# Projection front with ten unscaled k tiles, spread rescaling, and the last token tile ended in two halves

## The chip, the cores and the metric

The kernel runs on one core of a Trainium2 chip. The metric is the device time of one execution in microseconds, as the median of three runs. The times of the profile come from one further execution that was recorded instruction by instruction. PE is TensorE, DVE VectorE, ACT ScalarE, POOL GpSimd and SP SyncE, whose queue issues most of the transfers.

## The reference, cut to what matters

One decoder block on 512 tokens of width 2048. An RMS norm, one wide input projection, two token mixers (an mLSTM with 8 heads and a gated DeltaNet with 16 heads, both computed in chunks of 64 tokens), one output projection, and in the kernel's entry the residual and a last RMS norm.

```python
u = _rmsnorm(h, norm_w)                      # x * rsqrt(mean(x*x) + eps) * norm_w
proj = jnp.matmul(u, w_in)                   # q, k, v, o, z, gates of both mixers
i_pre = _softcap(ml_i + ml_i_bias)           # gates: 8 + 8 + 16 + 16 columns of proj
logf = jax.nn.log_sigmoid(_softcap(ml_f + ml_f_bias))
h_a = _mlstm_chunkwise(q, k, v, i_pre, logf) # then norm, sigmoid(o), silu(z)
beta = jax.nn.sigmoid(dn_b)
g = -jnp.exp(dn_a_log) * jax.nn.softplus(dn_a + dn_dt_bias)
h_b = _gated_delta_chunkwise(dq, dk_, dv_, beta, g)
y_a = jnp.matmul(h_a, w_out[:ML_WIDTH])
y_b = jnp.matmul(h_b, w_out[ML_WIDTH:])
return jax.nn.sigmoid(gate_a) * y_a + jax.nn.sigmoid(gate_b) * y_b
```

The factor rsqrt(mean(x*x) + eps) is one number for each token. It can be put on x before the projection, or on the projection's result.

## The kernel before

**Products in parts.** Each float32 operand is split into a high part rounded to fp32r and the rest: u into `uh` and `ul`, a weight tile `wr` into `wh` (a cast on ScalarE, L140) and `wl` (a subtraction on VectorE, L143). A product is three matmuls: uh with wh, ul with wh, uh with wl (L257 to L259). The 2048 input columns are 16 k tiles of 128; a weight tile holds 2 k tiles by 256 columns, 256 KB, and is loaded by SyncE (L172) in the order of a list `plan`. A projection block gives 256 columns for 512 tokens, in two banks `pj` of PSUM, with 96 matmuls of 512 columns.

**The front.** x comes in eight transfers of 512 KB, two halves for each of four tiles of 128 tokens (L270), ahead of the weights. For each token tile ScalarE squares one half and VectorE the other with a running sum (L297, L299); from these come the token factors `rs` (L301 to L304, the root on GpSimd), and both engines scale their half of x in place (L290, L292). Then `make_u` turns one k tile of x by four transposes (L313, tile `put`) and splits it into `uh` and `ul` (L314, L315), with the norm's weight as a factor by partition. `first_block` runs that two k tiles ahead of the first projection block (the mLSTM's queries), and puts between its products those of the gate columns (L324, L325, bank `pgr`), eight k tiles behind. At its end ScalarE copies the gates out (`gr0`, L356) and spills the queries (L349) to DRAM.

**Behind the front.** Three more projection blocks follow without a pause of TensorE. Beside them run generators that the blocks' `tick` calls step on. `gates()` transposes the gate columns back to tokens (L401, tile `pgt`), computes the decays on small columns `sml` in a long chain of VectorE instructions (L405 to L434), transposes these to rows (L443 to L445, tiles `pri`, `prf`, `prg`) and scans them (L454 to L457). `u_sums()` forms sums and differences of halves of u (L373 to L378, tile `X`, each k pair one pass of 1024 and four of 256 columns) and splits them (L382 and L384). They feed the stage that takes most of the kernel's time (L578 to L580), which forms four block products by seven.

**Order.** TensorE's order is the order in which the code is written. On the other engines a scheduler orders by priorities when the program is built; after that every engine works its queue strictly in that order, and a waiting instruction holds all behind it.

**The tail.** The last block of the output projection ends token tile by token tile: for tile c the products of the last six k tiles (18 matmuls of 512 columns, L1391 to L1393, bank `py`), then `done_c(c)`: gate and residual on VectorE (L1692, L1693), square on ScalarE (L1694), the sum (L1696), the root on GpSimd (L1697), the first 1024 output columns scaled on ScalarE (L1699) and sent by SyncE (L1700). `leave(c)` scales the other 1024 columns on VectorE (L1705, L1706) and sends them by ScalarE's queue (L1707).

Of the kernel before, what the change touches and what calls it, by code (L numbers as in the profile page):

```python
# [15 lines left out]
P = 128  # L16
# [12 lines left out]
GLAG = 8  # L29
# [29 lines left out]
def hybrid_body(  # L59
# [91 lines left out]
    plan = [("i", (ML_Q, ML_K)[a] + b * NB, k) for a, b in QK for k in range(0, KT, KP)]  # L151
# [10 lines left out]
    limit = [nfront]  # L162

# [11 lines left out]
    def split_next():  # L175
        raw, nk, n = raws[len(parts)]
        with tc.high_priority(offset=2 * PRIO if len(parts) > SAHEAD else 0):
            hi = wp.tile([P, nk, n], F32R, tag="wh", name="wh", bufs=NSPL)
            lo = wp.tile([P, nk, n], F32R, tag="wl", name="wl", bufs=NSPL)
            with ExitStack() as first:  # L180
                if not parts:
                    first.enter_context(behind("V"))
                    first.enter_context(behind("A"))
                elif len(parts) == 1:
                    first.enter_context(tc.issue_after(done["V"]))
                    first.enter_context(tc.issue_after(done["A"]))
                split_hi(hi, raw)
                split_lo(lo, raw, hi)
        parts.append((hi, lo))

    def prepare(i):
        while len(raws) < min(limit[0], i + RAHEAD + 1):
            load_raw()
        while len(parts) < min(limit[0], i + SAHEAD + 1):
            split_next()
# [50 lines left out]
    def proj_cm(col0, before=None):  # L246
        ps = [psj.tile([P, S], F32, tag="pj", name="pj") for _ in range(2)]
        for kt0 in range(0, KT, KP):
            hi, lo = next_w("i", col0, kt0)
            if before is not None:  # L250
                for k in range(KP):
                    before(kt0 + k)
            for j in range(2):
                for k in range(KP):
                    kt = kt0 + k
                    wsl = slice(j * P, (j + 1) * P)
                    T.matmul(ps[j], hi[:, k, wsl], uh[:, kt, :], start=(kt == 0), stop=False)  # L257
                    T.matmul(ps[j], hi[:, k, wsl], ul[:, kt, :], start=False, stop=False)  # L258
                    T.matmul(ps[j], lo[:, k, wsl], uh[:, kt, :], start=False, stop=(kt == KT - 1))  # L259
# [6 lines left out]
    xts = []  # L266
    for c in range(NC):
        xt = p0.tile([P, D], F32, tag=f"x{c}", name=f"xt{c}")
        for i in range(2):
            nc.sync.dma_start(xt[:, i * HD:(i + 1) * HD], x[c * P:(c + 1) * P, i * HD:(i + 1) * HD])  # L270
        xts.append(xt)
    for _ in range(2):
        load_raw()
# [3 lines left out]
    wgh, wgl = wgp[:, :, 0:48], wgp[:, :, 64:112]  # L277
    G.memset(wgp[:, :, 48:64].bitcast(F32), 0.0)
    taps = []
    ss = p0.tile([P, NC, 2], F32, tag="ss", name="ss")  # L280
    rs = p0.tile([P, NC], F32, tag="rs", name="rs")
    mhalf = cp.tile([P, NC], F32, tag="mhalf", name="mhalf")
    G.memset(mhalf, -0.5)
    half = cp.tile([P, 2, NC], F32, tag="half", name="half")
    G.memset(half, 0.5)
    sq, done = {}, {}

    def scale_x(c):
        with tc.issue_after(sq["V"]):
            newest["V"] = V.tensor_scalar(out=xts[c][:, 0:HD], in0=xts[c][:, 0:HD], scalar1=rs[:, c:c + 1], scalar2=None,  # L290
                                        op0=ALU.mult).ins
        newest["A"] = A.mul(xts[c][:, HD:D], xts[c][:, HD:D], rs[:, c:c + 1]).ins  # L292

    for c in range(NC):
        xt = xts[c]
        jk = p0.tile([P, HD], F32, tag="jk", name="jk", bufs=2)
        A.activation(jk, xt[:, 0:HD], AF.Square, accum_out=ss[:, c, 0:1])  # L297
        jv = p0.tile([P, HD], F32, tag="jv", name="jv", bufs=2)
        sq["V"] = V.scalar_tensor_tensor(out=jv, in0=xt[:, HD:D], scalar=1.0, in1=xt[:, HD:D], op0=ALU.mult, op1=ALU.mult,  # L299
                                         accum_out=ss[:, c, 1:2]).ins  # L300
        V.tensor_tensor(out=rs[:, c:c + 1], in0=ss[:, c, 0:1], in1=ss[:, c, 1:2], op=ALU.add)  # L301
        V.tensor_scalar(out=rs[:, c:c + 1], in0=rs[:, c:c + 1], scalar1=1.0 / D, scalar2=EPS,
                        op0=ALU.mult, op1=ALU.add)
        G.tensor_tensor(out=rs[:, c:c + 1], in0=rs[:, c:c + 1], in1=mhalf[:, c:c + 1], op=ALU.pow)  # L304
        if c:
            scale_x(c - 1)
    scale_x(NC - 1)

    def make_u(kt):
        pool, tg = ((psw, "wk"), (pso, "o"))[kt % 2]  # L310
        pt = pool.tile([P, S], F32, tag=tg, name="put")
        for c in range(NC):
            T.transpose(pt[:, c * P:(c + 1) * P], xts[c][:, kt * P:(kt + 1) * P], ident)  # L313
        done["A"] = A.activation(uh[:, kt, :], pt, AF.Copy, scale=normc[:, kt:kt + 1]).ins  # L314
        done["V"] = V.scalar_tensor_tensor(out=ul[:, kt, :], in0=pt, scalar=normc[:, kt:kt + 1],  # L315
                                           in1=uh[:, kt, :].bitcast(F32), op0=ALU.mult, op1=ALU.subtract).ins

    UA = 2
# [1450 lines left out]
```

## Time and profile before

| | us |
|---|---|
| median of three runs | 2154.34 (2153.77 to 2154.91) |
| the profiled execution's own time | 2153.98 |
| its span, first to last instruction | 2152.2 |
| PE busy | 2122.7 (99%) |
| DVE busy | 1710.5 (79%) |
| ACT busy | 1041.6 (48%) |
| first product of the first block | 20.64 |
| last product of the kernel | 2142.57 |

Busy time is the union of an engine's instructions; it says nothing of which engine the end waits for. The span is 1.8 us shorter than the execution's own time, since what precedes the first and follows the last instruction is not in it. In rows of the timeline the first number is an instruction's start from the span's begin, the second its duration; instructions of one engine overlap a little, so that the next one may start before the duration is over. The granted clock (PEclk) is a share of TensorE's full 2.4 GHz.

### The profile page before, as it was taken

Reading aid. Unit: us, or ns where it says so; the run is one execution under the profiler, and the core shown is the slowest. Engines: PE = TensorE matmul, PEld = TensorE weight load, DVE = VectorE, ACT = ScalarE, POOL = GpSimd, SP = SyncE. Lnnn points to the kernel's source line nnn. Section 1 sums busy time; section 2 is a strip of 40 time slices with the busy share of each in tenths; the row PEclk is TensorE's granted clock in tenths of the full one; section 3 lists DMA queues with packets and bytes.
Section 4 is the critical chain, followed back from the end, with each engine's and each line's share of the span. In section 5 each row is a group of like instructions: output and inputs, shape, how many; then the busy total and the mean of one; then the engine's idle time right before and its main releaser. Section 6 shows DMA issues by size and latency. Waiting matters only on the chain.

```text
span 2152.2 us, 31876 instructions
## 1 busy us (share of the span) xinstructions
PE 2122.7 (99%) x10544; PEld 1760.0 (82%) x10544; DVE 1710.5 (79%) x2973; ACT 1041.6 (48%) x1994; POOL 431.5 (20%) x651
## 2 busy tenths in 40 slices
PE   6999999999999999999999999999999999999998
PEld 5888888888888888888888888888888888887886
DVE  5888888788888778777757887887887878569887
ACT  5444444445444444444445545556455464345345
POOL 0000000000004000000002335234233263233221
PEclk9999999999999999999999999999999999999999
DMA  5456676667678767776767777767786677778895
GB/s 162 117 193 191 211 215 196 220 202 227 203 228 243 243 195 223 237 231 195 254 201 176 186 178 185 166 181 188 178 222 171 167 183 209 198 231 278 242 301 230
DMA packets 447143, 444.20 MB, mean 206 GB/s; under 512 B 197121, under 2 KB 303842, under 8 KB 446850
## 3 DMA queue, kind: packets, MB, share of 16 engines
q1 hardware_dynamic: 377618, 337.22, 54.7%
q0 software_dynamic: 24752, 72.90, 10.9%
q10 hardware_dynamic: 44608, 32.06, 4.7%
q8 instruction: 82, 1.34, 0.3%
q14 instruction: 83, 0.68, 0.1%
HBM read 348.66 MB, written 97.58 MB: 207 GB/s over the span
## 4 chain that ended last, share of the span: by engine, by line
PE 94%; DMA 2%; DVE 2%; SPq 1%; issue 1%; ACT 0%; ACTq 0%; DVEq 0%; POOLq 0%; POOL 0%
PE ps L579 17%; PE ps L578 17%; PE ps L580 17%; PE pj L257 9%; PE pj L259 9%; PE pj L258 9%; PE py L1391 2%; PE py L1393 2%; PE py L1392 2%; PE pk L909 1%; PE pqk L979 1%; PE pnum L1197 1%; PE pw L1071 1%; PE po L1086 1%; DMA wr<-in_w_in_dram 0%
## 5 line engine op out<-in xcount | busy, mean ns | idle before, releaser
L140 ACT CAST wh<-wr 128x512 fp32r<-128x512 f32 (+1 forms) x522 | 373.7, 717 | 442.3 <-PE pj L258 233.7
L143 DVE TENSOR_TENSOR wl<-wr,wh 128x512 fp32r<-128x512 f32 (+1 forms) x522 | 439.2, 842 | 171.5 <-ACT wh L140 167.6
L257 PE MATMUL pj<-uh,wh 128*128 128x512 f32 x896 | 376.4, 420 | 0.0
L259 PE MATMUL pj<-uh,wl 128*128 128x512 f32 x896 | 351.3, 392 | 0.0
L258 PE MATMUL pj<-ul,wh 128*128 128x512 f32 x896 | 350.6, 391 | 0.0
L579 PE MATMUL ps<-wl,uh 128*128 128x512 f32 x752 | 292.6, 389 | 0.0
L578 PE MATMUL ps<-wh,uh 128*128 128x512 f32 x752 | 292.6, 389 | 0.0
L580 PE MATMUL ps<-wh,ul 128*128 128x512 f32 x752 | 292.5, 389 | 0.0
L140 ACT CAST wh<-t 128x1024 fp32r<-128x1024 f32 x120 | 126.3, 1053 | 298.4 <-PE ps L580 189.9
L578 PE MATMUL ps<-wh,suh 128*128 128x512 f32 x624 | 242.9, 389 | 0.1
L579 PE MATMUL ps<-wl,suh 128*128 128x512 f32 x624 | 242.8, 389 | 0.0
L580 PE MATMUL ps<-wh,sul 128*128 128x512 f32 x624 | 242.7, 389 | 0.0
L533 POOL DMA_DIRECT2D t_d<-ts x104 | 56.6, 545 | 922.3 <-DVE ts L520 854.0
L140 ACT CAST wh<-ts 128x512 fp32r<-128x512 f32 x240 | 148.4, 618 | 186.8 <-DVE ts L538 157.6
L143 DVE TENSOR_TENSOR wl<-t,wh 128x1024 fp32r<-128x1024 f32 x120 | 146.9, 1224 | 82.1 <-ACT wh L140 81.6
L259 PEld LDWEIGHTS pj<-uh,wl 128*128 128x128 f32 x896 | 168.4, 188 | 37.3
L257 PEld LDWEIGHTS pj<-uh,wh 128*128 128x128 f32 x896 | 169.3, 189 | 30.1
L258 PEld LDWEIGHTS pj<-ul,wh 128*128 128x128 f32 x896 | 169.5, 189 | 28.3
L143 DVE TENSOR_TENSOR wl<-ts,wh 128x512 fp32r<-128x512 f32 x240 | 164.5, 686 | 32.8 <-ACT wh L140 31.3
L579 PEld LDWEIGHTS ps<-wl,uh 128*128 128x128 f32 x752 | 141.2, 188 | 29.7 <-DVE wl L143 0.4
L578 PEld LDWEIGHTS ps<-wh,uh 128*128 128x128 f32 x752 | 141.1, 188 | 29.4
L580 PEld LDWEIGHTS ps<-wh,ul 128*128 128x128 f32 x752 | 141.1, 188 | 29.1
(334 smaller groups left out, 3763.8 us busy)
## 6 DMA issues: line engine op xcount, KB each, us to landing
wr<-in_w_in_dram SPq DMA_DIRECT2D x744, 256.0 KB, 3.7
wr<-in_w_out_dram SPq DMA_DIRECT2D x138, 256.0 KB, 4.7
t_d<-ts POOLq DMA_DIRECT2D x104, 256.0 KB, 3.7
wr<-t_d SPq DMA_DIRECT2D x104, 256.0 KB, 3.8
xt<-in_x_dram SPq DMA_DIRECT2D x8, 512.0 KB, 7.1
tg_d<-X ACTq DMA_DIRECT2D x16, 256.0 KB, 4.7
tg_d<-to ACTq DMA_DIRECT2D x16, 256.0 KB, 4.4
v<-v_d SPq DMA_DIRECT2D x8, 512.0 KB, 6.1
```

The source lines that it names most:

```text
L140: newest["A"] = A.copy(hi, src).ins
L143: newest["V"] = V.tensor_tensor(out=lo, in0=src, in1=hi.bitcast(F32), op=ALU.subtract).ins
L257: T.matmul(ps[j], hi[:, k, wsl], uh[:, kt, :], start=(kt == 0), stop=False)
L258: T.matmul(ps[j], hi[:, k, wsl], ul[:, kt, :], start=False, stop=False)
L259: T.matmul(ps[j], lo[:, k, wsl], uh[:, kt, :], start=False, stop=(kt == KT - 1))
L533: queue.dma_start(t2_d[b % 2, i], ts[:, 0, :])
L578: T.matmul(ps[t], ah, hi, start=(g == "A" and i == 0), stop=False, skip_group_check=True)
L579: T.matmul(ps[t], ah, lo, start=False, stop=False, skip_group_check=True)
L580: T.matmul(ps[t], al, hi, start=False, stop=(i == KH - 1), skip_group_check=True)
L1391: T.matmul(ps[c], uh[:, kt, tsl], hi, start=(kt == ks[0]), stop=False)
L1392: T.matmul(ps[c], uh[:, kt, tsl], lo, start=False, stop=False)
L1393: T.matmul(ps[c], ul[:, kt, tsl], hi, start=False, stop=(kt == ks[-1]))
```

## The change

**Front.** x is one tile `xt` for all tokens and is loaded in five pieces of columns (borders 0, 256, 512, 1024, 1280, 2048), with the first weight tiles between them. The first `KU` = 10 k tiles are transposed and split unscaled and go into banks of their own (`rawp`, `rawg`). The squares stand in three pieces of columns between the steps of the first block (`hook`), on both engines in an order that the code writes out. When `rs` is there, x of k tiles 10 to 15 is scaled in place (`scale_x`), and the factors are turned into a row of tokens `rrow` by four matmuls (`turn_row`). With it the unscaled banks are brought to scale as they leave (`gr0`, `qk0`), and the second banks are added. `uh` and `ul` of the first ten k tiles are formed anew for the blocks that follow, pair by pair (`rescale`: sum and factor, `rescaled`: split); for k tiles 4 to 9 the transposed x is kept for that in the place of x in `xt`, which takes one more pass of ScalarE. The second block takes its k tiles in the order 10 to 15, 0 to 9. `gates()` starts four ticks later.

**Tail.** The products of the last token tile's last six k tiles are written in two halves of 256 columns, `done_c` runs for each half, and `whole(c)` scales the first 1024 columns in two pieces; the last tile leaves in four transfers of 256 KB, three by SyncE and one by ScalarE's queue.

The diff, cut to its core:

```diff
+KU = 10
+    KS = {q: list(range(0, KT, KP)) for q in QK}
+    KS[QK[1]] = list(range(KU, KT, KP)) + list(range(0, KU, KP))
...
-        xt = p0.tile([P, D], F32, tag=f"x{c}", name=f"xt{c}")
+    xt = p0.tile([P, NC, D], F32, tag="x", name="xt")
+    XC = [0, 256, 512, 1024, 1280, D]
+    for n in range(len(XC) - 1):
+        o = slice(XC[n], XC[n + 1])
+        with behind("S") if n else ExitStack():
+            newest["S"] = nc.sync.dma_start(xt[:, :, o], xv[:, :, o]).ins
+        if n in (0, 1, 3, 4):
+            with behind("S"):
+                load_raw()
...
+    def turn_row(diag):
+        pr = psw.tile([P, S], F32, tag="wk", name="prow")
+        for c in range(NC):
+            T.matmul(pr[:, c * P:(c + 1) * P], ones, diag[:, c, :], start=True, stop=True)
+        A.copy(rrow, pr)
...
+    def split_u(kt, pt):
+        hi, lo = uh[:, kt, :], ul[:, kt, :]
+        if kt < 4 or kt >= KU:
+            A.activation(hi, pt, AF.Copy, scale=normc[:, kt:kt + 1])
+            V.scalar_tensor_tensor(out=lo, in0=pt, scalar=normc[:, kt:kt + 1], in1=hi.bitcast(F32), op0=ALU.mult, op1=ALU.subtract)
+        else:
+            f = whole(kt - 4, 1)[:, 0]
+            A.activation(f, pt.rearrange("p (c t) -> p c t", t=P), AF.Copy, scale=normc[:, kt:kt + 1])
+            split_hi(hi.rearrange("p (c t) -> p c t", t=P), f)
+            split_lo(lo.rearrange("p (c t) -> p c t", t=P), f, hi.rearrange("p (c t) -> p c t", t=P))
+    def rescale(p):
...
+        if p < 2:
+            f = uf[p] = by_chunk(p0.tile([P, KP, S], F32, tag="uf", name="uf", bufs=2))
+            V.tensor_tensor(out=f, in0=hi.bitcast(F32), in1=lo.bitcast(F32), op=ALU.add)
+        else:
+            f = uf[p] = whole(KP * p - 4, KP)
+        V.tensor_tensor(out=f, in0=f, in1=rr, op=ALU.mult)
...
+    def hook(n):
...
+        if n == 7:
+            split_hi(wgh, wg)
+            split_lo(wgl, wg, wgh)
+            square(A, 2, 2)
+            square(V, 2, 3)
+            token_factors()
+        if n == 8:
+            scale_x(KU, KU + 2)
+            gps["diag"] = factor_row()
...
+        if n + 2 < KT:
+            split_u(n + 2, turn_x(n + 2))
...
+        if n in (11, 13, 15):
+            rescale((n - 11) // 2)
+        if n in (12, 14):
+            rescaled((n - 12) // 2)
...
+    with tc.manual_schedule(engines={mybir.EngineType.Activation, mybir.EngineType.DVE}):
...
+        gsum = V.tensor_tensor(out=gr0, in0=gr0, in1=gps["p"][0:112, :], op=ALU.add).ins
+    with behind("A"), tc.issue_after(gsum):
+        rescaled(2)
+        rescale(3)
+        rescale(4)
+        rescaled(3)
+        rescaled(4)
...
-    start(gates())
+    start(gates(), 4)
...
+        c = NC - 1
+        for n, at in ((slice(0, NB), 2), (slice(NB, NO), 3)):
+            for kt in tail:
+                products(ps, kt, c, *tw[kt], ks, n, True)
+            tick()
+            done_c(c, n, at)
+        whole(c)
         leave(2, 3)
         leave(3, 3)
```

TensorE in the first block, before: the last products of a pair of k tiles (`pj`), then the transposes of the pair ahead (`put`, of x tiles that are already scaled), in the same order for every pair.

```order
L257 MATMUL pj<-uh,wh 128x512
L258 MATMUL pj<-ul,wh 128x512
L259 MATMUL pj<-uh,wl 128x512
L313 MATMUL put<-ident,xt_108 128x128
L313 MATMUL put<-ident,xt_111 128x128
L313 MATMUL put<-ident,xt_114 128x128
L313 MATMUL put<-ident,xt_117 128x128
L313 MATMUL put<-ident,xt_108 128x128 [waits PE_49]
```

After, the same engine at step n = 8, where x is first needed scaled: the four transposes of k tile 10, the products of k tiles 8 and 9, and the first gate products.

```order
L331 MATMUL put<-ident,xt 128x128 [waits DMAHW0_49,Activation_49]
L331 MATMUL put<-ident,xt 128x128 [waits DVE_49]
L331 MATMUL put<-ident,xt 128x128 [waits Activation_49]
L331 MATMUL put<-ident,xt 128x128 [waits DVE_49]
L443 MATMUL pj<-uh,wh 128x512
L444 MATMUL pj<-ul,wh 128x512
L445 MATMUL pj<-uh,wl 128x512
L443 MATMUL pj<-uh,wh 128x512
L444 MATMUL pj<-ul,wh 128x512
L445 MATMUL pj<-uh,wl 128x512
L372 MATMUL pgr<-uh,wgp 112x512 [waits Pool_49]
```

The transposes now wait for the scaling of x on ScalarE and VectorE, and the products of two k tiles stand behind them without a wait of their own.

VectorE at the end of the gates' chain (`sml`, in before up to L434), before: the chain's last instructions, with one split of a weight (`wl`) and one group of the sums of u (`X`, `sul`, `s4l`) around them.

```order
L428 TENSOR_SCALAR sml<-sml 128x96 [waits DVE_49]
L143 TENSOR_TENSOR wl<-wr,wh 128x512 [waits DMAHW7_49,PE_49,Activation_49]
L429 TENSOR_TENSOR sml<-sml 128x96 [waits DVE_49]
L384 TENSOR_TENSOR sul<-X,suh 128x768 [waits Activation_49]
L430 SCALAR_TENSOR_TENSOR sml<-sml 128x96 [waits DVE_49]
L384 TENSOR_TENSOR s4l<-X,s4h 128x256 [waits Activation_49]
L431 TENSOR_SCALAR sml<-sml 128x4x8 [waits DVE_49]
L434 SCALAR_TENSOR_TENSOR sml<-sml 128x4x16
```

After, VectorE in the middle of that chain (its lines are now L537 to L552).

```order
L545 TENSOR_TENSOR sml<-sml 128x96 [waits DVE_49]
L491 TENSOR_TENSOR X<-uh,ul 128x1024 [waits DVE_49]
L143 TENSOR_TENSOR wl<-wr,wh 128x512 [waits DMAHW1_49,PE_49,Activation_49]
L546 TENSOR_SCALAR sml<-sml 128x96 [waits DVE_49]
L502 TENSOR_TENSOR sul<-X,suh 128x768 [waits Activation_49]
L502 TENSOR_TENSOR s4l<-X,s4h 128x256 [waits Activation_49]
L545 TENSOR_TENSOR sml<-sml 128x96 [waits DVE_49]
L143 TENSOR_TENSOR wl<-wr,wh 128x512 [waits DMAHW3_49,PE_49,Activation_49]
L493 TENSOR_TENSOR X<-X 128x256 [waits DVE_49]
L495 TENSOR_TENSOR X<-X 128x256
L546 TENSOR_SCALAR sml<-sml 128x96 [waits DVE_49]
```

Two groups of sums stood whole ahead of the chain's end before, four do so after, and the chain's instructions stand singly between them.

VectorE in the tail, before: the last passes of tile 2, the two of tile 3 (512 columns), and `leave(2)` (L1705, L1706) before the last addition.

```order
L1693 TENSOR_TENSOR hf<-X_19117,hf 128x512 [waits DVE_49]
L1696 TENSOR_TENSOR bia<-bia 128x1 [waits Activation_49]
L1692 SCALAR_TENSOR_TENSOR X_19117<-X_19117,py 128x512 [waits DMAHW5_49,PE_49]
L1693 TENSOR_TENSOR hf<-X_19117,hf 128x512 [waits DVE_49]
L1705 TENSOR_SCALAR hf<-hf,bia 128x512 [waits Pool_49]
L1706 SCALAR_TENSOR_TENSOR hf<-hf,bia,fw 128x512
L1696 TENSOR_TENSOR bia<-bia 128x1 [waits Activation_49]
```

VectorE in the tail, after: `done_c` of tile 2 (512 columns), both halves of tile 3 (256 columns), and `leave(2)` (L1829, L1830) between them.

```order
L1814 TENSOR_TENSOR hf<-X_19148,hf 128x512 [waits DVE_49]
L1813 SCALAR_TENSOR_TENSOR X_19148<-X_19148,py 128x256 [waits DMAHW2_49,PE_49]
L1814 TENSOR_TENSOR hf<-X_19148,hf 128x256 [waits DVE_49]
L1816 TENSOR_TENSOR bia<-bia 128x1 [waits Activation_49] x2
L1813 SCALAR_TENSOR_TENSOR X_19148<-X_19148,py 128x256 [waits PE_49]
L1814 TENSOR_TENSOR hf<-X_19148,hf 128x256 [waits DVE_49]
L1829 TENSOR_SCALAR hf<-hf,bia 128x512 [waits Pool_49]
L1830 SCALAR_TENSOR_TENSOR hf<-hf,bia,fw 128x512
L1816 TENSOR_TENSOR bia<-bia 128x1 [waits Activation_49]
```

TensorE there, after: the end of the first half and the begin of the second, which waits for VectorE.

```order
L1512 MATMUL py<-wh,uh 128x256
L1513 MATMUL py<-wl,uh 128x256
L1514 MATMUL py<-wh,ul 128x256
L1512 MATMUL py<-wth,uh 128x256 [waits DVE_49]
L1513 MATMUL py<-wtl,uh 128x256
```

In before there is one set of 18 such products of 512 columns and no wait in it.

## Rows read from the trace of the kernel before

**Rows 1.** The page: the chain that ended last, by engine.
```profile
PE 94%; DMA 2%; DVE 2%; SPq 1%; issue 1%; ACT 0%; ACTq 0%; DVEq 0%; POOLq 0%; POOL 0%
```
**Rows 2.** Waits of PE: what for, us in total, times, longest.
```profile
PE pprm L108 <- POOL rs L304: 14.5, 1, 14.5
PE put L313 <- DVE xt L290: 2.1, 2, 1.3
```
**Rows 3.** Timeline of the front: start us, duration us, engine, line, operation.
```profile
4.62 1.06 ACT L297 ACTIVATE jk<-xt 128x1024 f32<-128x1024 f32 x1 [2.59 <-DMA xt<-in_x_dram]
...
12.94 3.88 SPq L330 DMA_DIRECT2D wg<-in_w_in_dram  x1
...
14.24 1.22 DVE L299 SCALAR_TENSOR_TENSOR jv<-xt 128x1024 f32<-128x1024 f32 x1 [0.38 <-DMA xt<-in_x_dram]
...
17.95 3.03 PE L313 MATMUL put<-ident,xt 128*128 128x128 f32 x13 [1.28 <-DVE xt L290]
...
20.64 0.78 PE L257 MATMUL pj<-uh,wh 128*128 128x512 f32 x1
...
23.34 0.56 PE L257 MATMUL pj<-uh,wh 128*128 128x512 f32 x1
...
23.74 0.39 PE L258 MATMUL pj<-ul,wh 128*128 128x512 f32 x1
...
23.96 0.39 PE L259 MATMUL pj<-uh,wl 128*128 128x512 f32 x1
```
**Rows 4.** Windows: stretch, length, then busy us (count) of PE, PEld, DVE, ACT, POOL.
```profile
40.00:60.00 20.00, 20.00 (x100) 15.26 (x100) 6.97 (x14) 6.99 (x13) 0.61 (x2) 1.00 0.24 66
60.00:100.00 40.00, 40.00 (x184) 32.97 (x183) 37.00 (x82) 17.15 (x33) 0.00 (x0) 1.00 0.38 108
```
**Rows 5.** Timeline: the second block's first product, the gates' chain's end, its transposes.
```profile
57.17 0.40 PE L257 MATMUL pj<-uh,wh 128*128 128x512 f32 x1
...
79.58 0.22 DVE L434 SCALAR_TENSOR_TENSOR sml<-sml 128x64 f32<-128x64 f32 x1
...
86.20 0.27 PE L443 MATMUL pri<-ident,sml 128*8 128x128 f32 x1
```
**Rows 6.** Timeline of DVE from 66 to 71 us: passes of each width.
```profile
66.42 0.69 DVE L143 TENSOR_TENSOR wl<-wr,wh 128x512 fp32r<-128x512 f32 x1 [0.25 <-ACT wh L140]
67.03 1.22 DVE L373 TENSOR_TENSOR X<-uh,ul 128x1024 f32<-128x1024 f32 x1
68.17 0.25 DVE L427 TENSOR_TENSOR sml<-sml 128x96 f32<-128x96 f32 x1
68.34 0.42 DVE L375 TENSOR_TENSOR X<-X 128x256 f32<-128x256 f32 x1
68.67 0.42 DVE L377 TENSOR_TENSOR X<-X 128x256 f32<-128x256 f32 x1
...
70.69 0.95 DVE L384 TENSOR_TENSOR sul<-X,suh 128x768 fp32r<-128x768 f32 x1
```
**Rows 7.** Timeline of the tail: last product, VectorE's passes, the last root on POOL.
```profile
2140.82 0.68 DVE L1693 TENSOR_TENSOR hf<-X,hf 128x512 f32<-128x512 f32 x1
...
2142.57 0.39 PE L1393 MATMUL py<-wh,ul 128*128 128x512 f32 x1
...
2144.33 0.48 DVE L1705 TENSOR_SCALAR hf<-hf,bia 128x512 f32<-128x512 f32 x1
...
2144.73 0.74 DVE L1706 SCALAR_TENSOR_TENSOR hf<-hf,bia,fw 128x512 f32<-128x512 f32 x1
...
2145.62 0.55 POOL L1697 TENSOR_TENSOR bia<-bia,mhalf 128x1 f32<-128x1 f32 x1 [2.48 <-DVE bia L1696]
```
**Rows 8.** Windows behind the last product; PEclk is the last column but two.
```profile
2143.00:2146.00 3.00, 0.00 (x0) 0.00 (x0) 2.51 (x5) 1.87 (x3) 0.52 (x2) 1.00 0.65 265
2146.00:2147.00 1.00, 0.00 (x0) 0.00 (x0) 0.80 (x2) 0.80 (x1) 0.17 (x1) 0.88 1.02 418
2147.00:2148.00 1.00, 0.00 (x0) 0.00 (x0) 0.35 (x1) 0.35 (x1) 0.00 (x0) 0.50 0.67 274
```

More of the change, by code (lines that the diff above doesn't have):

```diff
@@ L179, in split_next @@
             lo = wp.tile([P, nk, n], F32R, tag="wl", name="wl", bufs=NSPL)
[L180 to L188, printed above, removed]
+            split_hi(hi, raw)
+            split_lo(lo, raw, hi)
         parts.append((hi, lo))
@@ L283, in hybrid_body @@
-    G.memset(mhalf, -0.5)
+    rrow = p0.tile([P, S], F32, tag="rrow", name="rrow")
     half = cp.tile([P, 2, NC], F32, tag="half", name="half")
     G.memset(half, 0.5)
[L286 to L306, printed above, removed]
@@ new lines, in square, with token_factors @@
+    def square(eng, n, c):
+        w = SQ[n].stop - SQ[n].start
+        xc, to = xt[:, c, SQ[n]], ss[:, c, n:n + 1]
+        if eng is V:
+            V.scalar_tensor_tensor(out=jv[:, 0:w], in0=xc, scalar=1.0, in1=xc, op0=ALU.mult, op1=ALU.mult, accum_out=to)
+        else:
+            A.activation(jk[:, 0:w], xc, AF.Square, accum_out=to)
+    def token_factors():
+        V.reduce_sum(out=rs, in_=ss, axis=mybir.AxisListType.X)
+        V.tensor_scalar(out=rs, in0=rs, scalar1=1.0 / D, scalar2=EPS, op0=ALU.mult, op1=ALU.add)
+        G.tensor_tensor(out=rs, in0=rs, in1=mhalf, op=ALU.pow)
@@ new lines, in scale_x, with factor_row @@
+    def scale_x(a, b):
+        for c in range(NC):
+            xc = xt[:, c, a * P:b * P]
+            if c % 2:
+                V.tensor_scalar(out=xc, in0=xc, scalar1=rs[:, c:c + 1], scalar2=None, op0=ALU.mult)
+            else:
+                A.mul(xc, xc, rs[:, c:c + 1])
+    def factor_row():
+        diag = p0.tile([P, NC, P], F32, tag="diag", name="diag")
+        for c in range(NC):
+            V.tensor_scalar(out=diag[:, c, :], in0=ident, scalar1=rs[:, c:c + 1], scalar2=None, op0=ALU.mult)
+        return diag
@@ new lines, in hook @@
+        if n == 8:
+            scale_x(KU, KU + 2)
+            gps["diag"] = factor_row()
+        if n in (9, 10):
+            for kt in range(KU // 2 * (n - 9), KU // 2 * (n - 8)):
+                gate_products(kt)
+        if n == 10:
+            turn_row(gps["diag"])
+        if n == 13:
+            turn_taps(*taps, psw)
+        if n + 2 < KT:
+            split_u(n + 2, turn_x(n + 2))
+        if n == 0:
+            square(A, 0, 0)
+        if n == 8:
+            scale_x(KU + 2, KT)
@@ new lines, in hybrid_body @@
+    with tc.manual_schedule(engines={mybir.EngineType.Activation, mybir.EngineType.DVE}):
+        pts = [turn_x(kt) for kt in range(2)]
+        split_u(0, pts[0])
+        split_next()
+        split_u(1, pts[1])
+        for j, p in enumerate(first_block()):
+            V.scalar_tensor_tensor(out=qk0[j], in0=p, scalar=QS, in1=qk0[j], op0=ALU.mult, op1=ALU.add)
+            nc.scalar.dma_start(qk_d[j], qk0[j])
+        gsum = V.tensor_tensor(out=gr0, in0=gr0, in1=gps["p"][0:112, :], op=ALU.add).ins
@@ L350, in spill @@
                 nc.scalar.dma_start(qk_d[o + j], t)
-    ps = proj_cm(ML_Q, before=first_block)
-    for kt in range(KT - GLAG, KT):
-        gate_products(kt)
-    gr0 = wp.tile([112, S], F32, tag="tg", name="gr0", bufs=3)
-    A.copy(gr0, pgr[0:112, :])
-    spill(ps, 0, float(P) ** -0.5)
     p0s.close()
@@ L1714, in last_block @@
             for c in range(NC):
-                products(ps, kt, c, *w, ks)
+                products(ps, kt, c, *w, ks, None, c == NC - 1, c == NC - 1 and kt == ks[KT - KLAST - 1])
                 if c % 2:
                     tick()
-        for c in range(NC):
+        for c in range(NC - 1):
             for n, kt in enumerate(tail):
```

176 lines of the change are left out of this document (115 added, 61 removed).

## The prediction

> **What bounds the kernel now.** I read the chain that ended last first: TensorE is 94% of it [rows 1]. So a change pays only where TensorE stands or starts late. The list of its waits then shows where that is: 14.5 us before its first instruction, and nothing else above 2.1 us [rows 2]. Between about 20.6 and 2143 us it does not stand, so there are two open places, the front (20.6 us until the first product) and the tail (from the last product, 2142.57, to the end of the span, 2152.2).
>
> In the front the reader is to see three things [rows 3]. The first 512 KB of x are there at 4.62 (ScalarE's first square waited for them), the last at 14.24, and the first product starts at 20.64, when the squares, the token factors and the scaling of all of x are done. The first products are slow: from the one at 20.64 to the seventh at 23.34 it is 0.45 us apiece, later 0.22 to 0.23 (23.74 to 23.96). That is TensorE at its lower and at its upper level, 1.2 and 2.4 GHz.
>
> Then I looked for what a faster front runs into. VectorE has room from 40 to 60 us (6.97 of 20 us busy), and little from 60 to 100 (37.00 of 40) [rows 4]. In the full stretch stands the chain on the gates' small columns (L416 to L434). It ends at 79.8, and TensorE's transposes that need it (L443) come at 86.20: 6.4 us of slack [rows 5].
>
> **The change, part by part: the early start.** x comes in five column pieces, of which the first holds two k tiles for all tokens and has the 512 KB whose landing the rows show. With the table of instructions that precede it (8 transposes, one cast, one split) I put the first product at 7.8 instead of 20.64: 12.8 us earlier. This is the offer; the rest is what is paid back.
>
> **First price: the token factors come late.** Ten k tiles go ahead unscaled, then TensorE's queue holds transposes of scaled x for k tile 10, ahead of the products of k tiles 8 and 9, which need nothing new. Scaled x needs the squares of all columns, and these now stand in the queues of ScalarE and VectorE between the splits of the weights and of u. From k tile 4's split (about 15.6, when ScalarE and VectorE are through the earlier k tiles) VectorE has nine subtractions of 512 columns at 0.60, five squares of 768 at 0.95, the gate weights' split at 0.87, small ones: 11.2 us. ScalarE has 12.5 us beside it, and each k tile goes to and fro between the two, some 2 us of hand-overs. The factors are there at 29.0, TensorE restarts at 29.5. It has used up k tiles 0 to 7 by 24.7 (from 7.8 on 48 products at 0.227 and 28 transposes at 0.109, 13.9 us, with 1.6 for a slow start like that of before and 1.4 of short waits). So it stands 4.9 us. The first block's last product ends at 52.4 instead of 57.17 [rows 5]: 4.8 of the 12.8 us are left.
>
> **Second price: VectorE's queue.** What was computed with unscaled x is repaired afterwards, nearly all of it on VectorE: five pairs of k tiles of uh and ul, each one or two passes of 1024 columns before the split and one in it, and the join of the two banks. From the rows [rows 6] (starts of neighbours, as 67.03 to 68.17 for 1024 columns): 12 passes of 1024 at 1.14 = 13.7 us, six of 512 at 0.66 = 4.0, together 17.7 us that were not there or were ScalarE's. They stand ahead of the gates' chain, and in the new order two more groups of sums of u (L491 to L502, 3.7 us each) and seven more splits of weights come ahead of the chain's end too: 7.4 and 4.2 us. VectorE now has, from k tile 12's split, which can start at 39.7 (29.5, then 32 products and gate products at 0.227, 16 small ones at 0.109, and two passes of ScalarE), to the end of the chain:
> 18 splits of 512 x 0.60 = 10.8; 16 passes of 1024 x 1.14 = 18.2; 4 of 768 x 0.87 = 3.5; 20 of 256 x 0.33 = 6.7; 10 of 512 with PSUM or a factor x 0.66 = 6.6; the small ones 5.7; together 51.5, and 2.4 for results that one instruction awaits of the one before. So the chain ends at 93.6. TensorE, from 52.4, has 144 products (32.7 us) and a stand of 1.5 us at the first transposes of the gates (L519), which now wait for the join of the gate banks behind the rescaling; it comes to the transposes of the columns (L562) at 87.1 and stands 6.5 us. The slack of 6.4 us of before is more than used.
>
> Set against before: there TensorE comes to these transposes at 86.20 with 18 products fewer behind it, 4.1 us at 0.227, so at equal work it is at 90.3. After, 93.6: **3.3 us later**, although the first block ended 4.8 earlier. From there to the tail the order is the same on every engine, and before has no stand there that a later arrival would shorten, so what is lost here stays.
>
> **Third price: the clock after a stand.** After the last product of the kernel the granted clock is 1.00 until 2146, then 0.88, then 0.50 [rows 8]: 1.2 GHz after 3.5 to 4 us of nothing to do. The two new stands are 4.9 and 6.5 us. After the second I count a restart at the lower level. The rows of before have one start at the lower level: work without a gap from 17.95, slow until 23.34 [rows 3], 5.4 us, half of which is lost: 5.4 x (1 - 0.227/0.45) = 2.6; I take **2.5 us**, bounds 0 and 2.7. After the first, 4.9 us are so near to the 3.5 to 4 that I leave it out of the sum; it would add another 2.4, since VectorE's 54 us start after it. The Trainium skill ("TensorE: Matmul & The Clock Gate", section "HAM oscillation — how this bites in real kernels") says that a long enough wait between groups of products makes every group start throttled. By that rule both stands cost a restart and the sum is 2162.5; the tail's rows agree on the fall, and no row of before shows a stand in mid-kernel.
>
> **The tail.** The last token tile's products go in two halves of 256 columns: 36 at 0.113 for 18 at 0.227, so no work is added. The first half ends at 2140.9, 2.0 us early. But both halves lie in one PSUM tile, and the order gives the second half's first product a wait for VectorE's read of the first. VectorE is busy with tile 2 until 2141.43 (L1693, 2140.82 + 0.61), reads 2141.5 to 2141.95, so TensorE stands 1.1 us and ends at 2144.2 instead of 2142.96. Then passes of 256 columns (0.42 for the 0.68 of 512), and tile 2's leaving (two passes of 512, 0.40 and 0.66 to the next start) still stands between them and the last addition: the root on GpSimd starts at 2146.3 instead of 2145.62 [rows 7]. Behind it ScalarE's 1024 columns are cut into two, so the first transfer leaves 0.6 earlier after the root, and the four transfers of 256 KB end together: 0.3 us later than before, bounds -0.8 (the transfers start as soon as the first half is out) and +1.2 (the last issue decides). The Trainium skill ("PSUM — Partial Sum Buffer", "Summary: rules for kernel authors") asks that a reader of PSUM beside a running product is in another bank; that speaks against halves in one bank. By it the stand is needed here, by a second bank the tail would gain 1.3 us instead of losing 0.3.
>
> **Sum.** The profiled execution took 2153.98 (span 2152.2), 0.4 under the median. 2153.98 + 3.3 + 2.5 + 0.3 = 2160.1; I say 2160.2.
>
> **Rivals.**
> 1. *A restart after both stands*: + 2.4, 2162.6. For it: 4.9 is above 4. Against: barely.
> 2. *No restart at all*: 2157.6. Against: the tail.
> 3. *The front's passes are quicker than the rows* and the squares are through when TensorE needs them (rs 4.9 us earlier): the whole front moves up by 4.9, the stand at L562 stays: -1.6 + 2.5 + 0.3, 2155.2. For it: before, squares and scaling of all of x took no more than 14 us. Against: there they had the engines for themselves.
> 4. *Faster, VectorE is not in the way.* Place: L562. If VectorE's and ScalarE's passes are a fifth shorter than the rows, the chain ends before TensorE comes and the first stand shrinks to 1.5: -4.1 and with the tail's -0.8, 2149.1; a tenth shorter would still leave +1. It decides from about 15% on. For it: nothing in the rows but that ScalarE shares the passes; against: the spacings of 0.60 and 1.14 [rows 6] are those of full queues, not of empty ones.
> 5. *The clock does not rise in the starved start*, so the products stay at 0.43 until 32 us: k tile 10 comes at 34.3, VectorE's 54 us start 4.8 later, 2165. For it: TensorE starts with a few transposes and waits.
> 6. *The loads don't come as written*: in before one issue of gate weights holds SyncE's queue for 3.88 us [rows 3]. If all loads after the first come 3 us later, it costs 1.7; it hides in the stand at k tile 10.
>
> **Chances.** Forecast 0.40; rival 1 0.24; rival 2 0.12; rival 3 0.08; rival 4 0.06; rival 5 0.10; rival 6 lies inside these. A difference within 0.2% (4.3 us) can't be told from none. Faster is rival 4: 0.06; the same are rivals 2 and 3: 0.20; slower 0.74. The range reaches from rival 3 (2155) to rival 5 (2165); outside lie rival 4, half of rival 5 and a little of rival 3, under 0.2.
>
> **What would show it.** Right: first product near 8; a stand of TensorE near 25 to 29 that ends with x scaled; a stand of 5 to 8 us at L562, released by VectorE's small columns, with VectorE busy 95% from 40 to 94; products of 0.4 us spacing behind it; a stand of 1 us before L1512's second half. Wrong: no wait at L562, or VectorE idle between 60 and 90. Then VectorE's sum is the step that failed. If the first block ends before 48, the token factors were costed too dear.

## The result, and the profile after

The changed kernel takes 2164.09 us (median of five runs, 2162.39 to 2166.15), the kernel before 2154.89 beside it: 1.0044 of its time, interval 1.0033 to 1.0056, 9.2 us slower. The profiled execution is the longest of the five (2166.15, span 2164.3).

The waits of PE in the trace of after (what for, us in total, times, longest) have, among others, these four in the place of [rows 2]:

```profile
PE prf L562 <- DVE sml L549: 6.3, 1, 6.3
PE put L331 <- ACT xt L313: 5.4, 1, 5.4
PE put L331 <- DMA xt<-in_x_dram: 3.6, 2, 2.0
...
PE py L1512 <- DVE X L1813: 0.9, 1, 0.9
```

Timeline of after, PE and POOL (start, duration, engine, line, operation, wait), to be read against [rows 3] and [rows 5]:

```profile
4.75 1.97 PE L331 MATMUL put<-ident,xt 128*128 128x128 f32 x8 [2.05 <-DMA xt<-in_x_dram]
8.30 1.12 PE L331 MATMUL put<-ident,xt 128*128 128x128 f32 x4 [1.58 <-DMA xt<-in_x_dram]
9.07 0.78 PE L443 MATMUL pj<-uh,wh 128*128 128x512 f32 x1
...
29.53 1.33 POOL L305 TENSOR_TENSOR rs<-rs,mhalf 128x4 f32<-128x4 f32 x1 [27.74 <-DVE rs L304]
...
31.45 1.12 PE L331 MATMUL put<-ident,xt 128*128 128x128 f32 x4 [5.37 <-ACT xt L313]
...
56.96 0.39 PE L250 MATMUL pj<-uh,wh 128*128 128x512 f32 x1
...
97.60 0.38 PE L562 MATMUL prf<-ident,sml 128*8 128x128 f32 x1 [6.29 <-DVE sml L549]
```

The first product comes at 9.07 instead of 20.64, 11.6 us sooner. The second block begins at 56.96 instead of 57.17: nearly all of it is gone within the first block. The transposes of the gates' columns wait until 97.60, where before had them at 86.20 with 18 products (4.1 us) less behind it: at equal work 7.3 us late. Between 1150 us (the first `pk` product of the mixers) and the late kernel nothing moves: after is 8.3 us late at the first, 7.9 at 1822.

The clock around the two stands, in windows of after (stretch, length, busy us and count of PE, PEld, DVE, ACT, POOL, then PEclk):

```profile
28.00:29.00 1.00, 0.00 (x0) 0.00 (x0) 0.90 (x4) 0.97 (x2) 0.00 (x0) 1.00 0.74 172
29.00:30.00 1.00, 0.00 (x0) 0.00 (x0) 0.93 (x3) 0.09 (x1) 0.47 (x1) 0.57 0.40 140
...
35.00:36.00 1.00, 1.00 (x4) 0.62 (x3) 0.69 (x1) 0.02 (x1) 0.00 (x0) 0.51 0.00 0
36.00:37.00 1.00, 1.00 (x5) 0.59 (x4) 0.00 (x0) 0.00 (x0) 0.00 (x0) 1.00 0.27 26
...
93.00:94.00 1.00, 0.00 (x0) 0.00 (x0) 1.00 (x6) 0.49 (x1) 0.00 (x0) 1.00 0.48 72
94.00:95.00 1.00, 0.00 (x0) 0.00 (x0) 0.97 (x3) 0.65 (x2) 0.00 (x0) 0.50 0.54 191
...
100.00:101.00 1.00, 1.00 (x4) 0.79 (x4) 1.00 (x2) 0.29 (x1) 0.00 (x0) 0.59 0.00 0
101.00:102.00 1.00, 1.00 (x6) 0.80 (x5) 1.00 (x2) 0.00 (x0) 0.00 (x0) 1.00 0.00 0
```

The first stand begins at 26.08, the clock is at half by 30 and full again by 36; the second begins at 91.31, half from 94 to about 100.8. So both stands have a restart at 1.2 GHz behind them.

VectorE behind the first stand, timeline of after: the split of k tile 12, from which on it is hardly without work, and the chain's end.

```profile
44.17 0.75 DVE L345 SCALAR_TENSOR_TENSOR ul<-put,normc,uh 128x512 fp32r<-128x512 f32 x1 [4.35 <-ACT uh L344]
...
97.45 0.22 DVE L552 SCALAR_TENSOR_TENSOR sml<-sml 128x64 f32<-128x64 f32 x1
```

That is 53.5 us of VectorE's queue. Busy for 97% of them (15.25 us of 15.83 up to 60, 36.79 of 37.67 behind), it is full; the stretch from 60 to 97 us, against [rows 4]:

```profile
60.00:97.00 37.00, 30.55 (x137) 24.69 (x135) 36.19 (x78) 16.64 (x29) 0.61 (x2) 0.96 0.45 128
```

The tail of after, timeline of PE and POOL (the roots of tile 2 and of tile 3), against [rows 7]:

```profile
2153.35 0.39 PE L1512 MATMUL py<-wth,uh 128*128 128x256 f32 x1 [0.85 <-DVE X L1813]
```
```profile
2154.05 0.54 POOL L1820 TENSOR_TENSOR bia<-bia,mhalf 128x1 f32<-128x1 f32 x1 [3.05 <-DVE bia L1816]
...
2157.89 0.54 POOL L1820 TENSOR_TENSOR bia<-bia,mhalf 128x1 f32<-128x1 f32 x1 [3.30 <-DVE bia L1816]
```

The roots lie 3.84 us apart, in before 3.03 (2142.59 and 2145.62): 0.8 us later at the root. From the last root to the end of the span it is 6.4 us, before 6.6.

The span grew by 12.1 us, more than the median's 9.2. The rest lies late in this one execution: products that wait at 1946.7 and 1948.2 for weights that came late (0.62 and 1.44 us), and a clock of 0.72 from 1960 to 1966. It is looked at below.

### The profile page after: what moved, and what is told of

Same layout as the page of the kernel before. It is cut to its first block, busy times and chain, and to the rows that moved or that the text cites. A ratio compares the mean times of both kernels' runs of the same rounds, so it can differ in the third digit from the quotient of the medians.

```text
span 2164.3 us, 31957 instructions
## 1 busy us (share of the span) xinstructions
PE 2130.2 (98%) x10570; PEld 1764.3 (82%) x10570; DVE 1726.6 (80%) x2998; ACT 1045.3 (48%) x2008; POOL 428.4 (20%) x649
## 3 DMA queue, kind: packets, MB, share of 16 engines
q0 software_dynamic: 24752, 72.90, 10.9%
## 5 line engine op out<-in xcount | busy, mean ns | idle before, releaser
L250 PE MATMUL pj<-uh,wh 128*128 128x512 f32 x864 | 363.1, 420 | 0.0
L252 PE MATMUL pj<-uh,wl 128*128 128x512 f32 x864 | 338.3, 392 | 0.0
L251 PE MATMUL pj<-ul,wh 128*128 128x512 f32 x864 | 337.9, 391 | 0.0
L252 PEld LDWEIGHTS pj<-uh,wl 128*128 128x128 f32 x864 | 162.3, 188 | 36.0
L250 PEld LDWEIGHTS pj<-uh,wh 128*128 128x128 f32 x864 | 163.1, 189 | 28.7
L251 PEld LDWEIGHTS pj<-ul,wh 128*128 128x128 f32 x864 | 163.2, 189 | 27.0
```

What stands on the lines that cost most here:

```text
L250: T.matmul(ps[j], hi[:, k, wsl], uh[:, kt, :], start=(kt == ks[0]), stop=False)
```

## Experiments

The table gives the medians, each with the kernel before on the same chip; `pk` is the start of the mixers' first `pk` product in the trace (before: 1149.9).

| kernel | median us | before | ratio, interval | stand at L562 | `pk` |
|---|---|---|---|---|---|
| changed | 2164.09 | 2154.89 | 1.0044, 1.0033 to 1.0056 | 6.3 | 1158.2 |
| changed_again | 2164.97 | 2154.33 | 1.0053, 1.0037 to 1.0068 | 6.3 | 1159.6 |
| front_only | 2164.66 | 2153.92 | 1.0044, 1.0029 to 1.0059 | 6.3 | 1159.6 |
| tail_only | 2156.23 | 2153.92 | 1.0007, 0.9997 to 1.0016 | none | 1149.2 |
| put_late | 2163.99 | 2153.92 | 1.0042, 1.0027 to 1.0057 | 6.3 | 1157.5 |
| sums_late | 2159.65 | 2153.92 | 1.0025, 1.0015 to 1.0034 | none | 1152.8 |
| norescale | 2160.53 | 2154.18 | 1.0029, 1.0019 to 1.0040 | 2.2 | 1155.1 |
| warm | 2162.66 | 2154.18 | 1.0037, 1.0022 to 1.0052 | 0.9 | 1157.6 |
| warm_first | 2162.73 | 2154.33 | 1.0041, 1.0028 to 1.0055 | 6.3 | 1155.9 |
| bank | 2163.76 | 2154.18 | 1.0045, 1.0029 to 1.0062 | 6.3 | 1159.3 |
| mended | 2152.07 | 2154.18 | 0.9988, 0.9979 to 0.9997 | none | 1147.1 |
| mended_again | 2152.56 | 2154.33 | 0.9995, 0.9987 to 1.0004 | none | 1147.7 |

Four profiles have the changed kernel's front as it is or with only the tail altered (changed, changed_again, front_only, bank): `pk` at 1158.2 to 1159.6. A difference under 1.5 us in that column is no finding by itself.

### front_only and tail_only: which half costs

front_only takes the products, `done_c` and `leave` of the last block from before; tail_only is before with those of the change:

```diff
-        for n, at in ((slice(0, NB), 2), (slice(NB, NO), 3)):
-            for kt in tail:
-                products(ps, kt, c, *tw[kt], ks, n, True)
-            tick()
-            done_c(c, n, at)
```

> The new front with the tail of before. Theory (the front's two stands of TensorE and a restart at 1.2 GHz behind each cost about 8.3 us, the tail 0.7): 8.3 us over before, about 2163; stands of 5.4 us at k tile 10's transposes and 6.3 at L562, products 0.43 us apart behind both. Rival (the tail or something in the late kernel is what costs): under 3 us over before.

> The front of before with the new tail. Theory: the second half's first product waits about 0.9 us for VectorE's read of the first half; the last root starts 0.7 to 0.8 us later against the last products of tile 2, the time is 0.3 to 0.9 us over before, which can hardly be told from none. Rival (the halves pay): 0.5 to 1.3 us under before. Rival (the tail is the loss): 5 us or more over before.

front_only is as slow as the whole change. tail_only is 2.3 us over before by the medians, with an interval that holds no difference. Its trace has the wait that was expected, and the same distance of the roots (3.83) as the changed kernel:

```profile
PE py L1395 <- DVE wl L143: 1.4, 1, 1.4
...
PE py L1394 <- DVE X L1695: 0.9, 1, 0.9
```

The front is the loss. The tail's rival of a gain falls; a loss of 0.8 us at the root fits, but is below what the times tell.

### put_late: the first stand

```diff
-        if n + 2 < KT:
+        if n + 2 < KT and n not in (8, 9):
             split_u(n + 2, turn_x(n + 2))
...
+            if n == 9:
+                for kt in (10, 11):
+                    split_u(kt, turn_x(kt))
+                scale_x(KU + 2, KT)
```

All twenty first gate products stand at n = 9, ahead of these transposes.

> The changed kernel with the transposes of k tiles 10 and 11 moved behind the products of k tiles 8 and 9 and the first twenty gate products, which need no scaled x. Theory (the first stand costs only through when VectorE can go on, since VectorE's queue sets L562): the stand of 5.4 us falls to pieces of 0.4 to 1.9 us with no restart at 1.2 GHz, but the stand at L562 stays at about 6.4 us with its restart: 2.3 us under the changed kernel, 6 to 7 over before. Rival (a stand costs what it lasts, so that its going is won whole): 7 us under the changed kernel, 1 to 2 over before.

The stand of 5.4 us is gone; the longest left is 1.48. Yet the stand at L562 is the same 6.3 us, from 90.63 on instead of 91.31, and `pk` is 0.7 to 2.1 us sooner than with the front unaltered. So the rival's 7 us did not come. The clock, though, did what the theory had not expected (windows of put_late):

```profile
27.00:28.00 1.00, 0.26 (x1) 0.00 (x0) 1.00 (x2) 1.00 (x3) 0.00 (x0) 1.00 1.09 337
28.00:29.00 1.00, 0.26 (x1) 0.26 (x1) 0.86 (x5) 0.66 (x2) 0.00 (x0) 0.73 0.79 251
29.00:30.00 1.00, 0.91 (x2) 0.41 (x3) 0.57 (x1) 0.00 (x0) 0.87 (x1) 0.50 0.11 38
```

It fell behind a stand of 1.48 us, and TensorE worked at half rate for 6.5 us (28.75 to 35.3), where it was 4.5 in the changed kernel. VectorE's split of k tile 12 starts at 43.48 instead of 44.17, and that difference is what L562 shows (96.91 instead of 97.60); but changed_again has 43.62 and 97.06 without any edit. So with the clock down nothing was won by the stand's going; what the stand alone is worth, this run can't show.

### sums_late: VectorE's order

```diff
-    start(u_sums(), 7)
+    start(u_sums(), 22)
```

> The changed kernel with the generator of the sums of u (u_sums) started at tick 22 instead of 7, so that its passes come behind the gates' chain on VectorE; nothing else is changed. Theory (VectorE's order, four groups of sums ahead of the chain's end, makes the stand at L562): no stand at L562 and no restart behind it, some 1.5 us of small waits for weights near 148 us in its place: 7.3 us under the changed kernel, 1.6 to 2.5 over before. Rival (the chain's own latency, or the rescaling ahead of it, sets L562): the stand keeps 4 us or more and the time falls by under 3. Rival (the sums then come too late for the block products): stands of several us between 100 and 150 us and no gain.

The gates' chain ends early, and the transposes come when TensorE does (timeline of sums_late, DVE and PE):

```profile
83.47 0.22 DVE L552 SCALAR_TENSOR_TENSOR sml<-sml 128x64 f32<-128x64 f32 x1
```
```profile
90.50 0.27 PE L562 MATMUL prf<-ident,sml 128*8 128x128 f32 x1
```

No stand, no fall of the clock behind it. In its place two waits for weights' splits at 142 and 149 us, 0.9 and 1.25 us. `pk` is 5.4 to 6.9 us sooner than in the four profiles with the unaltered front. By the medians it is 5.7 us over before, where the changed kernel is 9.2 and 10.6: a gain of 3.5 to 4.9, less than the 7.3 expected; its ten runs go from 2155.84 (the profiled one) to 2161.30, and what the slower of them lose was not recorded. The rivals fall: with all rescaling still in the queue the stand is gone, and the sums come early enough for the block products, but for 2 us.

### norescale: VectorE's sum

The pairs 3 and 4 of u stay unscaled, so the rest of the work uses unscaled values of k tiles 6 to 9.

```diff
         rescaled(2)
-        rescale(3)
-        rescale(4)
-        rescaled(3)
-        rescaled(4)
```

> The changed kernel without the rescaling of the pairs 3 and 4 (k tiles 6 to 9 of uh and ul stay unscaled for the blocks that follow, so two passes of factor and two of split of 1024 columns leave VectorE, 4.5 us, and two casts leave ScalarE). Theory (VectorE's sum ahead of the gates' chain sets L562): the stand of 6.3 us falls by 4 to 4.5 us, to about 2, and the time by 4 us if the clock still falls, by 6.7 if it does not. Rival (the chain's own latency sets it): the stand stays above 5.

```profile
PE prf L558 <- DVE sml L545: 2.2, 1, 2.2
```

4.5 us less in the queue, 4.1 us less stand. The clock still fell, so the time falls by the stand alone: `pk` by 3.1 to 4.5, the distance of the medians to before from 9.2 or more to 6.4. The queue's sum sets L562. The windows of norescale show when the clock fell:

```profile
94.00:95.00 1.00, 0.61 (x6) 0.48 (x7) 0.81 (x4) 0.00 (x0) 0.00 (x0) 1.00 0.61 124
95.00:96.00 1.00, 1.00 (x9) 0.90 (x7) 0.25 (x1) 0.40 (x1) 0.00 (x0) 0.75 0.40 138
96.00:98.00 2.00, 2.00 (x6) 1.52 (x6) 2.00 (x3) 0.17 (x1) 0.00 (x0) 0.50 0.00 0
```

The stand was over at 94.39, and the fall came at about 95.5, behind 1.1 us of the transposes. So here a restart followed a stand of only 2.2 us; whether the transposes had a part in it is not shown.

### warm and warm_first: the restarts

Unused products fill the stands; nothing else changes. warm:

```diff
+        for _ in range(24):
+            T.matmul(pri, uh[:, KT - 1, 0:P], uh[:, KT - 1, :], start=True, stop=True)
         for c in range(NC):
             tsl = slice(c * P, (c + 1) * P)
             T.transpose(pri[0:MLH, tsl], cf[:, c, 0:8], ident)
```

> The changed kernel with 24 more products of 512 columns, whose result is not used, ahead of the first transpose of the gates' columns (L561); nothing is taken away. At 0.227 us they fill 5.4 of the 6.3 us of the stand at L562. Theory (the stand's second cost is the fall of the clock behind it): the granted clock stays 1.00 through 90 to 102 us, the rest of the stand is about 0.9 us, and the time is 2 to 2.5 us under the changed kernel although there is more work. Rival (the clock's fall costs nothing that a later wait would not take anyway): the same time as the changed kernel.

> The changed kernel with 22 more products of 512 columns, whose result is not used, ahead of the transposes of k tile 10; they fill 5.0 of the first stand's 5.4 us, nothing is taken away. Theory (a restart at the lower clock behind the first stand delays VectorE's queue and so L562): the granted clock stays 1.00 through 26 to 40 us, the first block ends about 2 us sooner, L562 is released about 2 us sooner with the same stand of 6.3, the time is 2 us under the changed kernel. Rival (only VectorE's own passes set L562, from the factors on): L562 is released as before and the time stays.

warm_first does the same with 22 products in `turn_x` at kt = KU. The windows, of warm and then of warm_first:

```profile
94.00:98.00 4.00, 3.61 (x17) 2.66 (x15) 3.79 (x15) 1.14 (x2) 0.00 (x0) 1.00 0.25 66
98.00:102.00 4.00, 3.53 (x21) 2.88 (x22) 2.72 (x6) 0.58 (x1) 0.00 (x0) 1.00 0.00 0
```
```profile
26.00:32.00 6.00, 5.61 (x27) 4.25 (x26) 4.94 (x14) 3.77 (x8) 1.33 (x1) 1.00 0.40 122
32.00:36.00 4.00, 4.00 (x22) 2.86 (x21) 2.31 (x5) 2.42 (x4) 0.00 (x0) 1.00 0.00 0
```

In both the clock stays at 2.4 GHz where it was lost. In warm the transposes are released as late as ever (98.47), but from there to `pk` it is 1059.1 us instead of 1060.6 (changed) to 1062.6 (changed_again): 1.5 to 3.5 us. In warm_first it is 10.9 us from k tile 10's transposes to VectorE's split of k tile 12, in the seven traces that keep the first stand 12.0 to 13.3; L562 is reached at 89.25 instead of 90.8 to 91.9 and stands the same 6.28 us, `pk` is 2.3 to 3.7 us sooner. More work and a sooner end: each restart costs about 2 us, and the clock's windows say why it is not the same each time. In the changed kernel's first profile TensorE works at half rate for 4.5 and 3.2 us behind the two restarts, in its second (changed_again) for 3.0 and 5.8; half of that is lost. By the medians against the kernel before, both are 8.4 to 8.5 us over it where the changed kernel is 9.2 and 10.6; the intervals overlap, so the size rests on the traces.

### bank: the tail's wait

The second half's products get a bank of their own, from the first k tile on.

```diff
+        halves.extend([ps[3], psj.tile([P, NO], F32, tag="pj", name="py")])
...
-            to, hi, lo = to[:, n], hi[:, n], lo[:, n]
+            to, hi, lo = halves[n.start // NB][:, 0:NB], hi[:, n], lo[:, n]
```

> The changed kernel with the second half of the last token tile's products in a PSUM bank of its own, from the first k tile on. Theory (the wait is for the bank's reader, 0.9 us, and moves the tail): no stand ahead of the second half, the last root 1.0 to 1.3 us earlier after the first products of that tile, the time 0.8 to 1.3 us under the changed kernel, hardly to be told by the times, clear in the trace. Rival (VectorE's queue sets the tail anyway): the root is under 0.4 us earlier.

No wait at the second half, and the roots 2.73 us apart instead of 3.84 (timeline of bank, POOL):

```profile
2151.08 0.54 POOL L1823 TENSOR_TENSOR bia<-bia,mhalf 128x1 f32<-128x1 f32 x1 [3.05 <-DVE bia L1819]
2153.81 0.54 POOL L1823 TENSOR_TENSOR bia<-bia,mhalf 128x1 f32<-128x1 f32 x1 [2.19 <-DVE bia L1819]
```

The root is 1.1 us earlier, but from it to the end it is 6.7 instead of 6.4 (SyncE's last issue takes 0.84 us instead of 0.41; why, no run shows), so the tail is 0.8 us shorter. The times don't tell it.

### changed_again: the late stands

> The changed kernel itself, on the same chip as the two that follow, and with a second profile. Theory: 8 to 10 us over before; in the trace the same stands (5.4 us at k tile 10's transposes, 6.3 at L562, 0.9 at the tail's second half). The waits for late weights near 1947 us of the first profile (2.1 us) are chance and come smaller or not at all; rival: they belong to the change and come again with 2 us.

```profile
PE py L1513 <- DVE wl L143: 1.1, 1, 1.1
```

The two stands and the tail's wait come again to 0.1 us. The wait for late weights near 1947 us comes with 1.1 us instead of 2.1. Over the traces it is 0.7 to 1.4 us in front_only, put_late, norescale, tail_only and warm_first too, 0.2 in mended and none in sums_late, warm, bank and mended_again, which hold both halves of the change, nor in the one trace of before. So it comes with either half and can be missing with both; what moves it was not settled, and the rival that the change brings it now and then is open.

What did not come again is the clock's timing (windows of changed_again):

```profile
30.00:31.00 1.00, 0.00 (x0) 0.00 (x0) 0.10 (x1) 0.00 (x0) 0.99 (x1) 1.00 0.02 6
31.00:32.00 1.00, 0.41 (x2) 0.30 (x3) 0.97 (x5) 0.91 (x2) 0.00 (x0) 0.58 0.00 0
...
34.00:35.00 1.00, 1.00 (x4) 0.73 (x4) 1.00 (x3) 1.00 (x3) 0.00 (x0) 0.71 0.00 0
...
95.00:96.00 1.00, 0.00 (x0) 0.00 (x0) 0.90 (x5) 0.00 (x0) 0.00 (x0) 1.00 0.00 0
96.00:97.00 1.00, 0.00 (x0) 0.00 (x0) 0.90 (x5) 0.00 (x0) 0.00 (x0) 0.51 0.00 0
...
102.00:103.00 1.00, 1.00 (x4) 0.81 (x3) 1.00 (x2) 0.00 (x0) 0.00 (x0) 0.58 0.00 0
```

The stands begin at 26.22 and 90.78; the clock falls 4.9 and 5.2 us later, where it was 3.1 and 2.7 in the first profile of the same kernel.

### mended: four edits

put_late with the squares of step 7 behind the split of k tile 9, all of x scaled in one go, sums from tick 18 and gates from tick 6, and the tail of bank.

> Four edits at once on the changed kernel: transposes of k tiles 10 and 11 behind the products and gate products that need no scaled x, with the squares of step 7 behind the split of k tile 9; scaling of x in one go; sums of u from tick 18 and the gates from tick 6; the second half of the tail in its own bank. Theory by sums of the rows: no stand above 1.3 us, 5 us under the kernel before if the clock stays up in the starved stretch from 25 to 30 us, 2.5 under it if the clock falls there as it did with the transposes moved alone. Rival (what VectorE has to do has to be paid somewhere before the block products by seven are fed): not faster than before, with stands between 100 and 150 us.

> The kernel mended at four places, again, in five rounds beside the changed one: 2 us under the kernel before (0.9990 of its time, interval below 1), 11 to 12 us under the changed one.

No stand above 0.7 us between 10 and 120 us, and the clock stays up in the starved stretch:

```profile
25.00:30.00 5.00, 4.08 (x14) 2.08 (x13) 4.03 (x7) 4.20 (x8) 0.00 (x0) 1.00 0.60 176
```

The second block begins at 52.04 and 53.10, where it was 56.3 to 57.8 in the traces with the first stand: with the clock kept up, 3 to 6 us were won in the first block. Which of the edits did how much was not taken apart. `pk` is 2.2 to 2.8 us ahead of before, and 11 to 12 us ahead of the changed front. mended takes 0.9988 of before's time, mended_again 0.9995 with an interval that holds 1, where one below 1 was expected. So it beats the changed kernel by 11 to 12 us, and before by about 2 by the medians, which the second set of runs does not tell from none. The rest of the expected 5 was not traced in full; what the two traces show of it is the start (the transposes of the second piece of x begin at 8.15 and 9.23 us) and waits for weights' splits at 126 and 144 us (1.1 and 0.5 in mended, 0.7 and 0.5 in mended_again).

## Why the prediction was right

**Direction and place** were right: slower, by VectorE's queue in front of L562, and the trace shows each step where it was put. The time came out 9.2 us over before, where the forecast was 6.2 and rival 1 8.6 (from 2154.0 to 2162.6). That 2164.09 still lies inside the range is luck in part: the upper end, 2165, was rival 5's, and rival 5 did not come.

**The early start**: put at 7.8, is 9.07. The working counted 8 transposes ahead of the first product. TensorE's order has 12, and the last four, of k tile 2, wait for the second piece of x until 8.30. The first product doesn't need them: its `uh` and `wh` were there at 7.10 (ScalarE's cast, 6.49 + 0.61).

**First price**: a stand of 4.9 from 24.7 was expected, 5.37 from 26.08 came, ended by the scaling of x as said. The factors were there at 30.9 instead of 29.0. The root on GpSimd took 1.33 us for four columns, where before has 0.55 for one. The rest goes mostly with the start: over the traces the factors move with the landing of the second piece (bank: transposes at 7.63, root at 29.15; front_only: 8.70 and 30.04).

**Second price**: 53.9 us of VectorE's queue from k tile 12's split to the chain's end; 53.5 came. A stand of 6.5 at L562; 6.3 came. norescale and sums_late show both parts of the sum: 4.5 us of passes less is 4.1 us of stand less, and without the sums of u in front there is no stand. The stand at the first transposes of the gates was 0.76 instead of 1.5. (The terms given for TensorE's arrival at L562 add up to 86.6, not 87.1, and those for its end in the tail to 2144.1, not 2144.2; the forecast rests on neither.) VectorE busy 95% from 40 to 94 was named as a sign; it was 48.62 of 54 us, 90%, since its queue began 4.5 us later than put.

**Third price: here a step failed.** I left the restart behind the first stand out of the sum, since 4.9 us were "so near to the 3.5 to 4" of the tail. The clock fell 3.1 us after that stand's beginning and 2.7 us after the second's. Rival 1 was the case. The rule of the Trainium skill ("TensorE: Matmul & The Clock Gate", section "HAM oscillation — how this bites in real kernels"), which was weighed as counting both stands, fits these windows. To let the tail's one fall decide between 4.9 and 6.5 us was the mistake: over the traces the fall came 2.2 to 5.2 us after a stand's beginning, and in norescale it came behind a stand of 2.2 us. Each restart cost about 2 us by warm and warm_first, near the 2.4 and 2.5 taken; by the windows of after, half of 4.5 and of 3.2 us, it was 2.3 and 1.6. With it the delay closes: k tile 12's split began 4.5 us later than put (1.9 for the factors, 2.3 for the restart left out, 0.3 not traced), VectorE's queue was 0.4 shorter, and the chain ended at 97.7 instead of 93.6.

**The tail**: a stand of 1.1, came 0.85; the root 0.7 later, came 0.8; the end 0.3 later, came 0.6 (0.8 at the root, 0.2 less behind it), within its bounds. That a bank of its own takes the wait away held; the gain of 1.3 was 0.8 in bank against the changed kernel, so about 0.2 against before: the root came 1.1 us earlier, and from it to the end it took 0.3 longer.

**Rivals 3 to 5** did not come: the passes of VectorE's queue took what the rows gave, 53.5 us for 53.9, and the products went at 0.23 us from about 12 us on. Rival 6's condition came, and worse: an issue of gate weights held SyncE's queue for 8.10 us from 9.86 on. But no wait of the first 32 us is for a weight's transfer.

## What to carry to other kernels

An engine that is idle in the stretch you change may be full in the next: before moving work to it, add up its queue as far as the first instruction that the bounding engine waits for, in the new order, with rows of before. Here 17.7 us of new passes and a changed order made 53.5 us of queue, and of the 11.6 us by which the first product came sooner 0.2 were left at the second block, while a later start of a helper generator (tick 22 instead of 7) was worth 5.4 to 6.9 us at `pk`. A stand also costs what follows it: count a restart for every stand of some microseconds. Here one followed a stand of 2.2 us too, and in put_late a stretch that was idle only in pieces.

## What the runs showed of the hardware

- The granted clock fell 3.1 and 2.7 us after the begin of the two stands in the changed kernel's first profile, 4.9 and 5.2 in its second; over all traces with such a stand it was 2.2 (warm_first) to 5.2. After the restart TensorE worked at half rate for 2.8 to 5.8 us. After the last product of before it fell after 3.5 to 4 us [rows 8].
- It also fell with no long stand: in put_late, with none over 1.48 us, TensorE was 0.72, 0.92, 0.26 and 0.26 us busy in the four microseconds from 25 to 29, and the clock was at half by 29. In norescale a stand of 2.2 us and 1.1 us of transposes went before the fall. In mended TensorE was 4.08 of 5 us busy from 25 to 30, and the clock stayed.
- A root (`pow`) on GpSimd took 1.33 us on 128x4 (1.03 in mended and mended_again) and 0.54 to 0.57 us on 128x1, but for one of 0.94 in the tail of every trace.
